# High weights against both halves of x in one product of 512 columns, from up tile 44 on

## The chip, the core and the metric

The kernel runs on one NeuronCore of a Trainium2 chip. Five engines run side by side, each through its own queue in order: TensorE (PE in the profile; its weight loads are listed apart, as PEld), VectorE (DVE), ScalarE (ACT), GpSimd (POOL) and SyncE (SP, which issues the DMAs). They wait for each other by semaphores only. The metric is the device time of one execution in microseconds (us). The kernel before took 2370.12 us, the median of three runs (2369.03 to 2374.41).

## The reference

A decoder trunk of two layers over 256 positions of width 1024. Each layer has a mixer (a gated linear recurrence, an RWKV-7 branch and a latent attention, merged by gates) and then a retrieval over 16,384 experts of one neuron each (PEER), each followed by a residual and a layer norm. The part that matters here is PEER:

```python
q = (xt @ w_query).reshape(T, PEER_HEADS, 2, PEER_HALF)
s1 = jnp.einsum('thd,nd->thn', q[:, :, 0], subkeys[0])
s2 = jnp.einsum('thd,nd->thn', q[:, :, 1], subkeys[1])
...                                    # top 16 of each, top 16 of their sums
gate = jax.nn.softmax(top.astype(jnp.float32), axis=-1).astype(x.dtype)
u = u_table[ib]
vv = v_table[ib]
act = jax.nn.gelu(jnp.einsum('thkd,td->thk', u, xb))
return jnp.einsum('thk,thkd->td', gb * act, vv)
```

All values are float32.

## The kernel before

The kernel gathers nothing: for all 256 tokens it computes the activations of all 16,384 experts, H = gelu(U x), multiplies them by a matrix of gates that is zero outside the chosen experts, and multiplies the result by V. U is 128 "up" tiles of 128 experts, V 128 "down" tiles of 128 experts.

To keep float32 accuracy on TensorE, each operand is split in two float32r halves: hi is the rounded value, lo the remainder. A product is then the sum of three: hi·hi, hi·lo, lo·hi. For x this is done once per layer part (`split`, L165 to L167): the transposed x lies in two SBUF tiles, `xth` and `xtl`, each 128 partitions x 8 blocks x 256 tokens (`new_xt`, L161). For a weight tile it is done on the way in (`stream`, L77 to L90): SP issues a DMA of 512 KB into one of 4 `raw` buffers (L82), ACT casts it to `hi` (L84), and POOL or DVE subtracts `raw - hi` into `lo` (L88); hi and lo have 3 buffers each.

An up tile is `up(e)` (L953): `project` streams the weight tile and issues, for each of 8 blocks k, three matmuls into one PSUM tile `mm` of 128 x 256 (2 banks are set aside for `mm`): L247 hi weights against xth, L248 hi weights against xtl, L249 lo weights against xth. That is 24 matmuls of 256 columns, each with its own weight load. ACT then takes the gelu from PSUM into H (L955). For e < 44 POOL computes lo, from tile 44 on DVE does, since in the first part DVE is busy with the top-16 searches.

From up tile 64 on, `weigh` (L1006) runs beside the up tiles: about every second tile DVE builds 0/1 masks (`oh` L1011, `eq` L1013, `go` L1016), PE multiplies them (16 small matmuls into `sm`, L1020), and DVE multiplies eight tokens' worth of H by the gates (L1023). Then `accumulate` (L253) runs the down tiles: H is split four tiles at a time into `ah2` and `al2` (which take the place of xtl and xth in SBUF, by the tags xb and xa), and each down tile is 12 matmuls of 512 columns (L262) into four PSUM banks `acc`.

Nobody writes the order of instructions out by hand: a scheduler places each engine's instructions by program order and by when buffers come free, and inserts the semaphores. An engine then runs its queue strictly in that order, so that an instruction that waits holds up all that stands behind it.

Of the kernel before, what the change touches and what calls it, by code (L numbers as in the profile page):

```python
# [12 lines left out]
F32R = mybir.dt.float32r  # L13
# [3 lines left out]
AF = mybir.ActivationFunctionType  # L17
# [5 lines left out]
S = 256  # L23
D = 1024
P = 128
# [20 lines left out]
def trunk(ctx, tc, x, xT, w_in, w_br, w_out, w_q, skT, uT, vt, prm, lora, g2, v1, v2, rgw, w_uq, w_ukv,  # L46
          lnp, rope, out):
    nc = tc.nc
    V, A, G, T = nc.vector, nc.scalar, nc.gpsimd, nc.tensor

    const = ctx.enter_context(tc.tile_pool(name="const", bufs=1))
# [6 lines left out]
    def nm(s):  # L58
        uid[0] += 1
        return f"{s}{uid[0]}"  # L60

    def ps(tag, bufs):
        return psum.tile([P, 512], F32, tag=tag, name=nm(tag), bufs=bufs)
# [4 lines left out]
    def pacc():  # L68
        return ps("acc", 4)

    def psm():
        return ps("sm", 2)
# [4 lines left out]
    def stream(src, eng=None, pair=None):  # L77
        if eng is None:
            eng = lo_engine[cnt[0] % len(lo_engine)]
            cnt[0] += 1  # L80
        raw = ring.tile([P, 1024], F32, tag="raw", name=nm("raw"), bufs=NRAW)
        nc.sync.dma_start(raw, src)  # L82
        hi = ring.tile([P, 1024], F32R, tag="hi", name=nm("hi"), bufs=NHI) if pair is None else pair[0]
        A.copy(hi, raw)  # L84
        lo = ring.tile([P, 1024], F32R, tag="lo", name=nm("lo"), bufs=NHI) if pair is None else pair[1]
        n = 512 if eng is G else 1024
        for c in range(0, 1024, n):
            eng.tensor_sub(lo[:, c:c + n], raw[:, c:c + n], hi[:, c:c + n].bitcast(F32))  # L88
        return hi, lo
# [46 lines left out]
    with tc.tile_pool(name="setup", bufs=1) as sb:  # L136
        def t8(n):
            return sb.tile([P, L, 4], F32, tag=n, name=n)
        la = pr[:, :, PC["la"]:PC["la"] + 4]
        ab, e, q, w, w2, acc, rl = (t8(n) for n in ("ab", "e", "q", "w", "w2", "acc", "rl"))  # L140
# [18 lines left out]
    state = {"x": [x[b * P:(b + 1) * P, :] for b in range(2)]}  # L159

    def new_xt():  # L161
        state["xth"] = const.tile([P, 8, S], F32R, tag="xa", name=nm("xth"))
        state["xtl"] = const.tile([P, 8, S], F32R, tag="xb", name=nm("xtl"))

    def split(hi, lo, src, scale=1.0):  # L165
        A.activation(hi, src, AF.Copy, scale=scale)  # L166
# [54 lines left out]
    def finish(b, i, ln, last):  # L221
        if not last:
            if b == 0:
                new_xt()
            transpose_x(b, ln[b])
        nc.sync.dma_start(state["dst"][b], ln[b])
        if b:
            state["x"] = state["dst"]

    def drain(g):  # L230

        while True:
            try:
                next(g)
            except StopIteration as e:
                return e.value

    def project(src, eng=None):
        return drain(projecting(src, eng))

    def projecting(src, eng=None):
        hi, lo = stream(src, eng)
        h3, l3 = hi.rearrange("p (k c) -> p k c", k=8), lo.rearrange("p (k c) -> p k c", k=8)
        pt = pmm()[:, :S]
        xth, xtl = state["xth"], state["xtl"]
        for k in range(8):
            T.matmul(pt, h3[:, k, :], xth[:, k, :], start=(k == 0), stop=False)  # L247
            T.matmul(pt, h3[:, k, :], xtl[:, k, :], start=False, stop=False)  # L248
            T.matmul(pt, l3[:, k, :], xth[:, k, :], start=False, stop=(k == 7))  # L249
            yield  # L250
        return pt
# [638 lines left out]
    def peer(l, hp):  # L890
# [14 lines left out]
        H = [early.enter_context(tc.tile_pool(name=f"h{l}", bufs=1)).tile([P, 64, S], F32, tag="H0", name=nm("H"))]  # L905
# [9 lines left out]
        def nxt(k, lst):  # L915
            cyc[k] = cyc.get(k, -1) + 1
            return lst[cyc[k] % len(lst)]
# [33 lines left out]
            prev = (h, q)  # L951

        def up(e):  # L953
            p = project(uT[l, e], G if e < 44 else V)
            A.activation(H[e // 64][:, e % 64, :], p, AF.Gelu_apprx_tanh)  # L955

        up(0)
        scores(*prev)
        for e in range(1, 24):
            up(e)  # L960
# [18 lines left out]
        for f in range(2):  # L979
            for h4 in range(4):  # L980
                hs = slice(4 * h4, 4 * h4 + 4)
                t = nxt("map", maps)
# [4 lines left out]
        for e in range(24, 44):  # L987
            up(e)
        for b in range(2):
            p = psm()  # L990
# [43 lines left out]
            up(64 + e)  # L1034
            weigh_some(0, e)

        ah2 = const.tile([P, 2, 4, S], F32R, tag="xb", name=nm("ah"))
        al2 = const.tile([P, 2, 4, S], F32R, tag="xa", name=nm("al"))
        last = l == L - 1
        begin_finish(last)  # L1040
        late, ln = ExitStack(), []
# [17 lines left out]
        late.close()  # L1059

    new_xt()
    for q in range(2):
        xt0 = ring.tile([P, 4, S], F32, tag="raw", name=nm("xt0"), bufs=NRAW)
# [72 lines left out]
```

## Time and profile before

| | us |
|---|---|
| runs of the kernel: median (lowest to highest) | 2370.12 (2369.03 to 2374.41) |
| the profiled execution: time on the device | 2366.64 |
| the profiled execution: span from first to last instruction | 2364.9 |
| PE busy in the span | 2261.8 (96%) |
| DVE busy | 1712.3 (72%) |
| ACT busy | 1036.5 (44%) |
| POOL busy | 378.2 (16%) |

The span holds, for each layer, the mixer, the up tiles and the down tiles. In the first layer the up tiles from 44 on and the gates' products lie between about 540 and 799 us, in the second between about 1727 and 1987 us; the down tiles follow until 1168 us and to the end. A busy share of PE says only that a matmul was in flight: matmuls are pipelined, each is shown about 0.28 us long (256 columns) or 0.39 us (512 columns), and the next starts long before that. The distance between two starts is what a matmul costs.

### The profile page before, as it was taken

The page shows a single profiled execution, that of the slowest core. Times are in us where ns is not written, and L with a number is a line of the kernel's source. Part 1 is how long each engine was busy: PE and PEld are TensorE (multiplying, and loading weights), DVE is VectorE, ACT ScalarE, POOL GpSimd, SP SyncE. Part 2 cuts the span into 40 slices and gives each one's busy share as a digit, 9 for nine tenths or more (in the row PEclk, how much of TensorE's full clock was granted, in tenths as well). Part 3 has the DMA queues.
Part 4 walks back from the last instruction along what each step waited for, and adds up shares of the span by engine and source line. Part 5 has one row for each costly group of instructions (what it writes and reads, how often), then busy time and mean ns, then how long its engine had stood idle before and what let it go on. Part 6 is the DMA issues. An engine that isn't in the chain of part 4 may idle for free.

```text
span 2364.9 us, 42121 instructions
## 1 busy us (share of the span) xinstructions
PE 2261.8 (96%) x17092; PEld 2060.4 (87%) x17092; DVE 1712.3 (72%) x3066; ACT 1036.5 (44%) x1461; POOL 378.2 (16%) x284
## 2 busy tenths in 40 slices
PE   7998979999999999999899889799999999999998
PEld 6988969999999988888788789699999999888886
DVE  6888678945777788755676985789446777887556
ACT  4662324444444444444355623244444444444443
POOL 0020017990000000000000100179910000000000
PEclk9998989999999999999999988899999999999999
DMA  5334334455555555656543343345555555556564
GB/s 186 125 126 147 128 109 152 162 177 187 170 168 164 169 178 170 213 194 195 184 142 125 107 131 112 110 145 168 171 187 173 167 167 173 169 170 215 194 191 139
DMA packets 104931, 382.02 MB, mean 162 GB/s; under 512 B 11648, under 2 KB 12160, under 8 KB 104480
## 3 DMA queue, kind: packets, MB, share of 16 engines
q1 hardware_dynamic: 104736, 379.32, 48.9%
q8 instruction: 134, 2.20, 0.4%
q14 instruction: 61, 0.50, 0.1%
HBM read 374.56 MB, written 4.72 MB: 160 GB/s over the span
## 4 chain that ended last, share of the span: by engine, by line
PE 88%; DVE 7%; issue 2%; POOL 2%; ACT 1%; DMA 0%; SPq 0%; DVEq 0%; POOLq 0%; ACTq 0%
PE acc L262 31%; PE mm L247 15%; PE mm L249 15%; PE mm L248 15%; PE sm L1020 3%; DVE lo L88 2%; POOL lo L88 2%; PE acc L812 1%; PE acc L813 1%; PE acc L811 1%; PE sm L932 1%; DVE ti L591 1%; DVE tmp L589 0%; PE sm L298 0%; PE acc L397 0%
## 5 line engine op out<-in xcount | busy, mean ns | idle before, releaser
L84 ACT CAST hi<-raw 128x1024 fp32r<-128x1024 f32 x658 | 689.8, 1049 | 1067.0 <-PE mm L248 439.8
L247 PE MATMUL mm<-xth,hi 128*128 128x256 f32 x3104 | 896.9, 289 | 14.5 <-ACT hi L84 10.9
L249 PE MATMUL mm<-xth,lo 128*128 128x256 f32 x3104 | 891.3, 287 | 15.7 <-POOL lo L88 9.8
L88 DVE TENSOR_TENSOR lo<-raw,hi 128x1024 fp32r<-128x1024 f32 x538 | 660.5, 1228 | 337.3 <-ACT hi L84 335.4
L248 PE MATMUL mm<-xtl,hi 128*128 128x256 f32 x3104 | 887.4, 286 | 0.0
L249 PEld LDWEIGHTS mm<-xth,lo 128*128 128x128 f32 x3104 | 600.5, 194 | 24.7 <-POOL lo L88 14.9
L247 PEld LDWEIGHTS mm<-xth,hi 128*128 128x128 f32 x3104 | 601.8, 194 | 19.9 <-ACT hi L84 10.9
L248 PEld LDWEIGHTS mm<-xtl,hi 128*128 128x128 f32 x3104 | 601.6, 194 | 2.8 <-issue 1.2
L88 POOL TENSOR_TENSOR lo<-raw,hi 128x512 fp32r<-128x512 f32 x240 | 342.8, 1458 | 418.3 <-ACT hi L84 255.1
L262 PE MATMUL acc<-hi,ah 128*128 128x512 f32 x1000 | 316.6, 396 | 0.5 <-ACT ah L166 0.5
L262 PE MATMUL acc<-lo,ah 128*128 128x512 f32 x1000 | 311.7, 391 | 0.0
L262 PE MATMUL acc<-hi,al 128*128 128x512 f32 x1000 | 310.0, 389 | 0.0
L262 PEld LDWEIGHTS acc<-hi,al 128*128 128x128 f32 x1000 | 187.7, 188 | 40.8
L262 PEld LDWEIGHTS acc<-lo,ah 128*128 128x128 f32 x1000 | 187.7, 188 | 40.5 <-DVE lo L88 0.2
L262 PEld LDWEIGHTS acc<-hi,ah 128*128 128x128 f32 x1000 | 183.1, 188 | 34.8 <-ACT ah L166 0.7
L1023 DVE SCALAR_TENSOR_TENSOR H<-sm,H 128x512 f32<-128x512 f32 x128 | 88.3, 690 | 85.1 <-PE sm L1020 84.4
L167 DVE SCALAR_TENSOR_TENSOR al<-H,ah 128x1024 fp32r<-128x1024 f32 x64 | 78.4, 1225 | 42.6 <-ACT ah L166 42.6
L517 POOL MEMSET rmask<- 128x1024 f32 x2 | 1.9, 954 | 663.3 <-DVE xtl L167 646.4
L166 ACT ACTIVATE ah<-H 128x1024 fp32r<-128x1024 f32 x64 | 67.8, 1060 | 80.5 <-PE acc L262 77.1
L1016 DVE TENSOR_TENSOR go<-eq,gp 128x512 f16<-128x512 f16 x256 | 97.3, 418 | 0.0
L955 ACT ACTIVATE H<-mm 128x256 f32<-128x256 f32 x256 | 96.5, 377 | 0.0
L1011 DVE TENSOR_TENSOR oh<-iota,ix 128x1024 f16<-128x1024 f16 x128 | 87.7, 685 | 2.3 <-PE sm L1020 2.3
(352 smaller groups left out, 2131.4 us busy)
## 6 DMA issues: line engine op xcount, KB each, us to landing
raw<-in_uT_dram SPq DMA_DIRECT2D x256, 512.0 KB, 3.4
raw<-in_vt_dram SPq DMA_DIRECT2D x256, 512.0 KB, 3.4
raw<-in_w_in_dram SPq DMA_DIRECT2D x100, 512.0 KB, 3.4
raw<-in_w_q_dram SPq DMA_DIRECT2D x32, 512.0 KB, 3.4
raw<-in_w_br_dram SPq DMA_DIRECT2D x24, 512.0 KB, 3.3
raw<-in_w_out_dram SPq DMA_DIRECT2D x16, 512.0 KB, 3.5
ln<-in_lnp_dram SPq DMA_DIRECT2D x8, 512.0 KB, 5.7
xd<-ln SPq DMA_DIRECT2D x6, 512.0 KB, 2.6
```

What stands on the lines that cost most here:

```text
L84: A.copy(hi, raw)
L88: eng.tensor_sub(lo[:, c:c + n], raw[:, c:c + n], hi[:, c:c + n].bitcast(F32))
L167: V.scalar_tensor_tensor(lo, src, scale, hi.bitcast(F32), op0=OP.mult, op1=OP.subtract)
L247: T.matmul(pt, h3[:, k, :], xth[:, k, :], start=(k == 0), stop=False)
L248: T.matmul(pt, h3[:, k, :], xtl[:, k, :], start=False, stop=False)
L249: T.matmul(pt, l3[:, k, :], xth[:, k, :], start=False, stop=(k == 7))
L262: T.matmul(acc[b][hf], m[:, bs], w[:, 512 * hf:512 * hf + 512], start=(k == 0 and j == 0), stop=(k == n - 1 and j == 2))
L955: A.activation(H[e // 64][:, e % 64, :], p, AF.Gelu_apprx_tanh)
L1011: V.tensor_tensor(oh, iota16[:, None].to_broadcast([P, 8, 64, 2]), ix[:, 1, tt, None, :].to_broadcast([P, 8, 64, 2]), op=OP.is_equal)
L1016: V.tensor_tensor(go[:, i], eq, gp[:, i, tt, None, :].to_broadcast([P, 8, 32, 2]), op=OP.mult)
L1020: T.matmul(p[:, j * 64:(j + 1) * 64], oh[:, j].rearrange("p a b -> p (a b)"), go[:, i, j].rearrange("p a b -> p (a b)"), start=(i == 0), s ...
L1023: V.scalar_tensor_tensor(hv, p.rearrange("p (t e) -> p e t", t=8), 1 / GATE_SCALE, hv, op0=OP.mult, op1=OP.mult)
```

## The change

From up tile 44 on, `up` no longer calls `project`. xth and xtl become the two halves of one tile `xt` (128 x 8 x 2 x 256), so that for each block k the 256 columns of xth and the 256 of xtl lie side by side. The hi weights of a block meet all 512 columns in one matmul (`high`), the lo weights meet the 256 of xth (`low`), whose result is added to the first half of the bank; that makes 8 matmuls of 512 and 8 of 256 columns per tile. The PSUM tile is now one of the four `acc` banks. Its second half holds hi·xtl: ACT copies it into H, DVE adds the first half, and ACT takes the gelu in place. For the same reason ah2 and al2 become halves of one tile under the same tag.

```diff
     def new_xt():
-        state["xth"] = const.tile([P, 8, S], F32R, tag="xa", name=nm("xth"))
-        state["xtl"] = const.tile([P, 8, S], F32R, tag="xb", name=nm("xtl"))
+        xt = state["xt"] = const.tile([P, 8, 2, S], F32R, tag="xab", name=nm("xt"))
+        state["xth"], state["xtl"] = xt[:, :, 0], xt[:, :, 1]
...
         def up(e):
-            p = project(uT[l, e], G if e < 44 else V)
-            A.activation(H[e // 64][:, e % 64, :], p, AF.Gelu_apprx_tanh)
+            if e < 44:
+                p = project(uT[l, e], G if e < 44 else V)
+                A.activation(H[e // 64][:, e % 64, :], p, AF.Gelu_apprx_tanh)
+                return
+
+            hi, lo = stream(uT[l, e], V)
+            h3, l3 = hi.rearrange("p (k c) -> p k c", k=8), lo.rearrange("p (k c) -> p k c", k=8)
+            p, xt = pacc(), state["xt"]
+            for k in range(8):
+                def high():
+                    T.matmul(p, h3[:, k, :], xt[:, k].rearrange("p a t -> p (a t)"), start=(k == 0), stop=(k == 7))
+
+                def low():
+                    T.matmul(p[:, 0:S], l3[:, k, :], xt[:, k, 0], start=False, stop=False)
+
+                for f in ((low, high) if k == 7 else (high, low)):
+                    f()
+            h = H[e // 64][:, e % 64, :]
+            A.copy(h, p[:, S:2 * S])
+            V.tensor_add(h, h, p[:, 0:S])
+            A.activation(h, h, AF.Gelu_apprx_tanh)
...
-        ah2 = const.tile([P, 2, 4, S], F32R, tag="xb", name=nm("ah"))
-        al2 = const.tile([P, 2, 4, S], F32R, tag="xa", name=nm("al"))
+        a2 = const.tile([P, 2, 2, 4, S], F32R, tag="xab", name=nm("a2"))
+        ah2, al2 = a2[:, 0], a2[:, 1]
```

On PE, two blocks k of an up tile in the first layer stood like this (mm is the tile's PSUM sum, hi and lo its weights):

```order
L247 MATMUL mm_6064<-xth_3551,hi_6060 128x256
L248 MATMUL mm_6064<-xtl_3552,hi_6060 128x256
L249 MATMUL mm_6064<-xth_3551,lo_6062 128x256
L247 MATMUL mm_6064<-xth_3551,hi_6060 128x256
L248 MATMUL mm_6064<-xtl_3552,hi_6060 128x256
L249 MATMUL mm_6064<-xth_3551,lo_6062 128x256
```

and of an up tile past 44 in the changed kernel, from its first block on (L964 is `high`, L967 is `low`):

```order
L964 MATMUL acc_6116<-xt_3550,hi_6112 128x512
L967 MATMUL acc_6116<-xt_3550,lo_6114 128x256
L964 MATMUL acc_6116<-xt_3550,hi_6112 128x512
L967 MATMUL acc_6116<-xt_3550,lo_6114 128x256
L964 MATMUL acc_6116<-xt_3550,hi_6112 128x512
L967 MATMUL acc_6116<-xt_3550,lo_6114 128x256
```

Three matmuls per block became two, with the same 768 columns.

On DVE, one period of two up tiles past tile 64 stood like this in the first layer (L1023 applies the gates, L88 makes lo of an up tile three ahead, oh, go and eq are the masks):

```order
L1023 SCALAR_TENSOR_TENSOR H_3591<-sm_6909,H_3591 128x64x8
L88 TENSOR_TENSOR lo_7020<-raw_7016,hi_7018 128x1024
L1011 TENSOR_TENSOR oh_7080<-iota_5923,ix_5925 128x1024
L1016 TENSOR_TENSOR go_7082<-eq_7081,gp_5927 128x512 x2
L1013 TENSOR_TENSOR eq_7227<-iota_5923,ix_5925 128x512
L88 TENSOR_TENSOR lo_7052<-raw_7048,hi_7050 128x1024
L1023 SCALAR_TENSOR_TENSOR H_3591<-sm_6998,H_3591 128x64x8
```

and so in the changed kernel (L973 is the added sum; L1042, L1030, L1035 and L1032 are L1023, L1011, L1016 and L1013 of before; acc_6789, acc_6840, acc_6866 and then the tile of lo_6915 follow each other on PE):

```order
L973 TENSOR_TENSOR H_6448<-H_6448,acc_6789 128x256
L1042 SCALAR_TENSOR_TENSOR H_3589<-sm_6816,H_3589 128x64x8
L88 TENSOR_TENSOR lo_6915<-raw_6911,hi_6913 128x1024
L1030 TENSOR_TENSOR oh_6886<-iota_5921,ix_5923 128x1024
L1035 TENSOR_TENSOR go_6888<-eq_6887,gp_5925 128x512 x2
L973 TENSOR_TENSOR H_6448<-H_6448,acc_6840 128x256
L1032 TENSOR_TENSOR eq_7092<-iota_5921,ix_5923 128x512
L88 TENSOR_TENSOR lo_6941<-raw_6937,hi_6939 128x1024
L973 TENSOR_TENSOR H_6448<-H_6448,acc_6866 128x256
```

The sum of tile n stands ahead of lo of tile n + 3; the rest kept its order. On ACT the copy of tile n now stands ahead of the cast of tile n + 3, and the gelu of tile n behind it. POOL and SP kept their order.

## Rows read from the trace of the kernel before

**Rows 1.** The page: engines' busy time, share of the span, instructions

```profile
PE 2261.8 (96%) x17092; PEld 2060.4 (87%) x17092; DVE 1712.3 (72%) x3066; ACT 1036.5 (44%) x1461; POOL 378.2 (16%) x284
```

**Rows 2.** The page: the chain that ended last, by engine and by line

```profile
PE 88%; DVE 7%; issue 2%; POOL 2%; ACT 1%; DMA 0%; SPq 0%; DVEq 0%; POOLq 0%; ACTq 0%
PE acc L262 31%; PE mm L247 15%; PE mm L249 15%; PE mm L248 15%; PE sm L1020 3%; DVE lo L88 2%; POOL lo L88 2%; PE acc L812 1%; PE acc L813 1%; PE acc L811 1%; PE sm L932 1%; DVE ti L591 1%; DVE tmp L589 0%; PE sm L298 0%; PE acc L397 0%
```

**Rows 3.** Busy us by stretch: length, PE, PEld, DVE, ACT, POOL, clock, DMA, GB/s

```profile
548.00:602.00 54.00, 54.00 (x453) 54.00 (x452) 24.07 (x23) 25.25 (x38) 0.00 (x0) 1.00 0.58 187
606.00:798.00 192.00, 192.00 (x1955) 190.67 (x1954) 146.00 (x220) 81.15 (x122) 0.00 (x0) 1.00 0.52 167
1792.00:1984.00 192.00, 192.00 (x1955) 190.67 (x1954) 147.15 (x220) 79.85 (x121) 0.00 (x0) 1.00 0.51 167
```

**Rows 4.** Groups by line, 606 to 798 us: busy, mean ns, idle before

```profile
L88 DVE TENSOR_TENSOR lo<-raw,hi 128x1024 fp32r<-128x1024 f32 x61 | 74.4, 1220 | 13.2 <-ACT hi L84 13.2
L84 ACT CAST hi<-raw 128x1024 fp32r<-128x1024 f32 x61 | 64.0, 1049 | 112.2 <-PE mm L248 112.2
L1023 DVE SCALAR_TENSOR_TENSOR H<-sm,H 128x512 f32<-128x512 f32 x31 | 21.4, 690 | 31.7 <-PE sm L1020 31.7
```

**Rows 5.** Timeline, PE: start us, us, instruction, at an up tile's end

```profile
619.85 0.28 PE L247 MATMUL mm<-xth,hi 128*128 128x256 f32 x1
...
621.77 0.28 PE L248 MATMUL mm<-xtl,hi 128*128 128x256 f32 x1
621.89 0.28 PE L249 MATMUL mm<-xth,lo 128*128 128x256 f32 x1
622.01 0.64 PE L1020 MATMUL sm<-go,oh 128*128 128x64 f16 x16
...
622.68 0.28 PE L248 MATMUL mm<-xtl,hi 128*128 128x256 f32 x1
```

**Rows 6.** Chain in order of time, down tiles of the first layer

```profile
982.57 185.37 PE acc L262 x816
```

**Rows 7.** Timeline, DVE, one period past tile 64, with idle before

```profile
620.28 1.23 DVE L88 TENSOR_TENSOR lo<-raw,hi 128x1024 fp32r<-128x1024 f32 x1 [0.36 <-ACT hi L84]
622.68 0.69 DVE L1023 SCALAR_TENSOR_TENSOR H<-sm,H 128x512 f32<-128x512 f32 x1 [1.17 <-PE sm L1020]
623.29 1.22 DVE L88 TENSOR_TENSOR lo<-raw,hi 128x1024 fp32r<-128x1024 f32 x1
624.42 0.69 DVE L1011 TENSOR_TENSOR oh<-iota,ix 128x1024 f16<-128x1024 f16 x1
625.03 0.75 DVE L1016 TENSOR_TENSOR go<-eq,gp 128x512 f16<-128x512 f16 x2
625.81 0.42 DVE L1013 TENSOR_TENSOR eq<-iota,ix 128x512 f16<-128x512 f16 x1
626.60 1.23 DVE L88 TENSOR_TENSOR lo<-raw,hi 128x1024 fp32r<-128x1024 f32 x1 [0.36 <-ACT hi L84]
```

**Rows 8.** Timeline, ACT, behind the end of the same up tile

```profile
622.09 1.05 ACT L84 CAST hi<-raw 128x1024 fp32r<-128x1024 f32 x1 [1.55 <-PE mm L248]
623.04 0.38 ACT L955 ACTIVATE H<-mm 128x256 f32<-128x256 f32 x1
```

**Rows 9.** Groups by line, whole span: nearest to copy and sum

```profile
L948 ACT COPY tk<-mm 128x256 f32<-128x256 f32 x32 | 11.7, 365 | 0.0
L817 DVE SCALAR_TENSOR_TENSOR gt<-gt,acc 128x256 f32<-128x256 f32 x16 | 6.7, 418 | 3.5 <-PE acc L813 3.4
L940 DVE TENSOR_TENSOR tk<-tk 128x256 f32<-128x256 f32 x32 | 27.6, 861 | 0.0
```

**Rows 10.** Timeline from the last up tile to the first down tile

```profile
799.33 0.96 PE L1020 MATMUL sm<-go,oh 128*128 128x64 f16 x27
799.41 1.06 ACT L166 ACTIVATE ah<-H 128x1024 fp32r<-128x1024 f32 x1 [1.55 <-PE mm L248]
...
800.52 0.50 PE L262 MATMUL acc<-hi,ah 128*128 128x512 f32 x1 [0.23 <-ACT ah L166]
```

## The prediction

> **What bounds the kernel now.** First the page's table of engines: PE is busy for 96% of the span, DVE for 72%, ACT for 44% [rows 1]. The chain that ended last agrees: 88% of it is PE, 45% the three projection lines L247 to L249, DVE 7% [rows 2]. Shares over the span hide stages, so the next view is the busy time by stretch. Within the changed part PE has no idle time: 54.00 of 54 us among tiles 44 to 63, 192.00 of 192 us among tiles 64 to 127, in both layers alike, at granted clock 1.00, the 2.4 GHz level [rows 3]. DVE is at 45% and then 76%, ACT at 47% and 42%, POOL is idle. The groups by line say who waits for whom: the casts wait for PE's matmuls (112.2 us), DVE's L1023 for PE's gate products (31.7 us), lo for the cast (13.2 us) [rows 4]. So everyone waits for PE here, and only PE's own time counts, as long as the others keep up.
>
> What a matmul costs is the distance of starts. With 256 columns, 16 starts take from 619.85 to 621.77 us: 120 ns each [rows 5]. With 512 columns, 816 matmuls of the down tiles take 185.37 us, of which the last one's shown length is 0.39: 184.98 / 815 = 227 ns [rows 6]. Two products of 256 columns cost 240 ns, one of 512 costs 227: 13 ns go with the instruction and not with its columns.
>
> **The change, part by part.**
> *PE, the matmuls.* A tile before: 24 x 0.120 = 2.880 us. After: 8 x 0.227 + 8 x 0.120 = 2.776 us. 104 ns less per tile, for 84 tiles in each of two layers: 168 x 0.104 = 17.5 us less. No row shows 512 and 256 columns taking turns, so the block's price is bounded from both sides. Above: the long one costs as much as two short ones, 360 ns as before, gain 0. Below: nothing but columns, 768 at the granted 2.4 GHz = 320 ns (an estimate from the clock of rows 3), 8 x 40 = 320 ns a tile, 53.8 us in all. I take 347, since both spacings stand in the trace over long unbroken stretches.
>
> The rows put 13 ns on each matmul beside its columns. The Trainium skill (TensorE: Matmul & The Clock Gate, section Back-to-back issue gap) gives columns / 2.4 + 2.5 ns between isolated matmuls at the full clock, that is 109 and 216 ns. By that rule the change would save an estimated 2.5 ns x 8 x 168 = 3.4 us, so it speaks against the change; the trace does not agree with it, at 120 and 227 ns.
>
> *ACT.* Per tile it gains a copy of 128 x 256 out of PSUM, 0.37 us by the nearest row (L948, 365 ns) [rows 9], and its gelu now reads SBUF instead of PSUM; I leave it at 0.38 [rows 8]. 0.37 + 1.05 + 0.38 = 1.80 us in 2.78: free of charge, hidden under PE.
>
> *DVE.* Per tile it gains a sum of 128 x 256 with one operand in PSUM. The nearest rows are 418 ns (L817, PSUM, same size) and, far off, 861 ns (L940, same size, both operands in SBUF and another shape of access) [rows 9]; from below no more than nothing. I take 0.42, since L817 reads PSUM in the same shape. In the period of two tiles DVE works without a gap from 622.68 to 626.23 (625.81 + 0.42), 3.55 us, and on one more lo of 1.23: 4.78 us; it waits 1.17 and 0.36 [rows 7]. With two sums 5.62. The new period on PE is 2 x 2.776 plus the gate product, 0.55 (622.01 to the 622.56 that lies one step ahead of the L248 at 622.68) [rows 5] = 6.10 us. DVE fits, at 92%.
>
> *The added waits.* The sum of tile n waits for ACT's copy, which waits for the last matmul of n. Behind it on DVE stand, in the order shown with the change, L1042 of the gate product and lo of tile n + 3; behind the gelu on ACT stands the next copy. Let tile n leave PE at 0. Its last matmul, shown 0.39 long, ends at 0.16; the cast of before began 0.04 after the shown end of the last L248 (621.77 + 0.28, 622.09) [rows 5, 8], so the copy runs from 0.20 to 0.57, the cast of n + 3 to about 1.6, the sum from 0.6 to 1.0. L1042 to 1.6, lo of n + 3 to 2.8, the masks to 4.15. The copy of n + 1 is done at 0.55 + 2.78 + 0.57 = 3.90, its sum ends at 4.57, the mask eq and lo of n + 4 (cast done at 4.9) end at 6.1. The next sum could not start before 6.10 + 0.60 = 6.70: DVE still idles 0.6 us per period. PE needs lo of n + 3 at 6.65 + 0.23 and lo of n + 4 at 9.4: 3 to 4 us in hand. lo of n + 3 could not be early anyway, since its buffer is that of tile n (three buffers), which is why the casts waited for PE before. So the waits cost nothing; without this cover each would cost 0.6 us a tile. PSUM: four acc banks instead of two mm banks, freed 1.0 us after a tile leaves PE; no wait.
>
> *DMA.* The order on SP did not move; raw buffers come free with lo, as before. 512 KB per 2.78 us instead of 2.88 is 4% more than the 187 GB/s of tiles 44 to 63 at a DMA share of 0.58 [rows 3]: hidden.
>
> *The seam to the down tiles.* The first split (ah) waited for the last L248 and began 0.08 us after tile 127 left PE at 799.33; the first down matmul came at 800.52, after 0.23 us idle [rows 10]. Now ACT does the copy of tile 127 first: ah from about 0.55 to 1.6, and the down tiles begin 1.63 instead of 1.19 us after the last up tile. Cost 0.44, twice: 0.9 us, bounded by 0 (if gate products fill it) and 2 x 1.2. xt and a2 now share one buffer, but both halves were released at the same end before.
>
> *Sum.* -17.5 + 0.9 = -16.6 us. The profiled execution took 2366.64 us (span 2364.9 and 1.7 around it) and would take 2350.0. It lies 3.5 us below the median of the runs, 2370.12; the forecast for a median is 2370.1 - 16.6 = 2353.5 us.
>
> **The rivals.**
> *No gain on PE (B).* The 13 ns may belong to the succession and not to the instruction: now each long product must cover the load of the low weights and each short one that of the high weights, and a stream that takes turns may fall back to 360 ns per block. For it: no row shows the mix, and PEld was at 99% of these stretches [rows 3]. Against it: loads are as many per matmul as before, and both pure streams carry the same 13 ns. Time 2370.1 + 0.9 = 2371. By the rule of the Trainium skill named above (TensorE: Matmul & The Clock Gate, section Back-to-back issue gap) it would be an estimated 2370.1 - 3.4 + 0.9 = 2367.6 us.
>
> *A larger gain (C).* If at 256 columns it is the weight load that sets 120 ns, then fewer loads free more: down to 320 ns per block, 2370.1 - 53.8 + 0.9 = 2317. For it: the loads fill PEld at 256 columns. Against it: at 512 columns, where loads have twice the room, the same 13 ns remain.
>
> *DVE becomes the bound (D, slower).* Place: tiles 64 to 127, 32 periods in each layer. The sum decides: above (6.10 - 4.78) / 2 = 0.66 us each, DVE is longer than PE and PE starts to wait for lo; above about 0.8 the loss eats what tiles 44 to 63 win (40 x 0.104 = 4.2). At L940's 0.86 the period is 4.78 + 1.72 = 6.50 instead of the present 6.32: 64 x 0.18 = 11.5 us lost, 2370.1 + 11.5 - 4.2 + 0.9 = 2378. If besides DVE's present waits (1.17 + 0.36) stayed on top of 5.62, the period would be 7.15 and the time 2420. For it: 92% in a queue that now waits twice more per period. Against it: these waits end with a tile whose successors' lo is already made, and L817's 418 ns is the same access.
>
> **How the numbers follow.** Forecast 77%, its own range 2349 to 2358 us (block price by 2 ns, seam, scatter of the runs); B 9%, C 5%, D 9%. About 0.2%, 4.7 us, is what a measurement of this kernel can tell from no change. Faster by more than that: the forecast and C, 82%. Within it: B, 9%. Slower: D, 9%. The range for 8 times in 10 takes the forecast and nearly all of B, and leaves C and D out: 2346 to 2371 us.
>
> **What would show it.** Right: in the stretch of tiles 44 to 127 PE is without idle time, L964 starts are followed after 227 ns and L967 after 120, so that a block takes 347 ns; DVE is near 90% in tiles 64 to 127 with the sum at about 0.42 us and still idle once per period, before the odd tile's sum, and the first down tile starts some 9 us earlier in the first layer and 17 in the second. Wrong: a block at 360 (B) or near 320 (C), or idle time of PE before L967 that ends with DVE's lo, with DVE never idle (D).

## The result, and the profile after

The changed kernel takes 2353.45 us (median of 8 runs, 2350.16 to 2358.08), the kernel before, run beside it, 2368.31 us (8 runs, 2357.90 to 2374.41). The ratio is 0.9939, 95% interval 0.9926 to 0.9952: 14.4 us less, between 11.4 and 17.5. The forecast was 2353.5 us. (One of all executions here, of experiment 1, ran at a granted clock of 0.83, took 2498.69 us and is left out of that experiment's ratio.) The profiled execution of the changed kernel took 2351.38 us, 15.3 less than that of before.

Line numbers of the changed kernel: L964 is the long product (512 columns), L967 the short one, L972 ACT's copy, L973 DVE's sum, L974 the gelu, L1042 the gate product's multiplication, L1011 the transposes just ahead of tile 44.

Engines on the page, against [rows 1]: 1344 matmuls fewer, PE still at 96%, DVE up from 72 to 75%.

```profile
PE 2247.3 (96%) x15748; PEld 1982.4 (84%) x15748; DVE 1764.3 (75%) x3234; ACT 1089.2 (46%) x1629; POOL 378.6 (16%) x284
```

Busy time by stretch (length, PE, PEld, DVE, ACT, POOL, clock, DMA share, GB/s), against [rows 3]: PE still has no idle time in the changed part, at granted clock 1.00. PEld fell from 99 to 87%, DVE rose from 76 to 88%.

```profile
548.00:600.00 52.00, 52.00 (x297) 45.21 (x296) 33.71 (x48) 30.46 (x56) 0.00 (x0) 1.00 0.56 184
604.00:788.00 184.00, 184.00 (x1465) 159.58 (x1465) 161.69 (x275) 97.88 (x180) 0.00 (x0) 1.00 0.53 172
1775.00:1965.00 190.00, 190.00 (x1499) 164.89 (x1498) 166.23 (x284) 101.56 (x186) 0.00 (x0) 1.00 0.52 172
```

Groups by line from 604 to 788 us, against [rows 4, 9]: no idle time ahead of L964 or L967. The copy costs 373 ns, the sum 417. The sum waits 18.0 us for the copy, no row shows a wait for the sum; L1042, 31.7 us idle before, now never waits.

```profile
L964 PE MATMUL acc<-xt,hi 128*128 128x512 f32 x477 | 170.1, 399 | 0.0
L967 PE MATMUL acc<-xt,lo 128*128 128x256 f32 x476 | 123.4, 279 | 0.0
L88 DVE TENSOR_TENSOR lo<-raw,hi 128x1024 fp32r<-128x1024 f32 x60 | 73.5, 1224 | 4.9 <-ACT hi L84 4.9
L973 DVE TENSOR_TENSOR H<-H,acc 128x256 f32<-128x256 f32 x60 | 25.0, 417 | 18.0 <-ACT H L972 18.0
L972 ACT COPY H<-acc 128x256 f32<-128x256 f32 x60 | 22.4, 373 | 86.8 <-PE acc L964 86.8
L1042 DVE SCALAR_TENSOR_TENSOR H<-sm,H 128x512 f32<-128x512 f32 x32 | 21.9, 684 | 0.0
```

DVE's timeline of one period answers to [rows 7]: idle time is left twice, 0.18 and 0.64 us.

```profile
620.16 1.23 DVE L88 TENSOR_TENSOR lo<-raw,hi 128x1024 fp32r<-128x1024 f32 x1
...
622.57 0.41 DVE L973 TENSOR_TENSOR H<-H,acc 128x256 f32<-128x256 f32 x1
622.90 0.42 DVE L1032 TENSOR_TENSOR eq<-iota,ix 128x512 f16<-128x512 f16 x1
623.51 1.23 DVE L88 TENSOR_TENSOR lo<-raw,hi 128x1024 fp32r<-128x1024 f32 x1 [0.18 <-ACT hi L84]
625.37 0.42 DVE L973 TENSOR_TENSOR H<-H,acc 128x256 f32<-128x256 f32 x1 [0.64 <-ACT H L972]
```

PE's timeline, two pieces of neighbouring tiles, answers to [rows 5]: blocks (a long and a short product) take 346 to 347 ns in the first (from 619.87, 620.22, 620.56), 349 to 361 in the second (from 622.65, 623.01, 623.36; the view rounds to 10 ns). The forecast had 347 everywhere.

```profile
619.87 0.39 PE L964 MATMUL acc<-xt,hi 128*128 128x512 f32 x1
620.10 0.28 PE L967 MATMUL acc<-xt,lo 128*128 128x256 f32 x1
620.22 0.39 PE L964 MATMUL acc<-xt,hi 128*128 128x512 f32 x1
620.45 0.28 PE L967 MATMUL acc<-xt,lo 128*128 128x256 f32 x1
620.56 0.39 PE L964 MATMUL acc<-xt,hi 128*128 128x512 f32 x1
...
622.65 0.40 PE L964 MATMUL acc<-xt,hi 128*128 128x512 f32 x1
622.89 0.28 PE L967 MATMUL acc<-xt,lo 128*128 128x256 f32 x1
623.01 0.40 PE L964 MATMUL acc<-xt,hi 128*128 128x512 f32 x1
623.25 0.28 PE L967 MATMUL acc<-xt,lo 128*128 128x256 f32 x1
623.36 0.40 PE L964 MATMUL acc<-xt,hi 128*128 128x512 f32 x1
```

**Where the time went.** The stretch from the transposes to the first down matmul holds all that was changed. Before, it ran from 539.05 to 800.52 us and from 1726.61 to 1988.07, 261.47 and 261.46 us; the same two rows of after, with the last gate products between them:

```profile
543.63 0.82 PE L1011 MATMUL sm<-ident,tk 128*128 128x128 f32 x6
...
797.42 1.11 PE L1039 MATMUL sm<-go,oh 128*128 128x64 f16 x32
799.00 0.50 PE L262 MATMUL acc<-hi,a 128*128 128x512 f32 x1 [0.47 <-ACT a L166]
```

255.37 us, and 255.37 again in layer 2 (1717.74 to 1973.11): 12.2 us less in both. The other 3.1 of the 15.3 us between the two profiled executions lie where the two programs do the same work: the first layer reaches its transposes 4.6 us later, the second needs 7.4 us less from its first down matmul to its transposes in the next layer, the end 0.3 less. The granted clock in such stretches changes from execution to execution (0 to 340 us: 0.96 before, 0.94 after), and the time goes with it: among the profiles of this case that do the same work up to there, the first transposes come at 537.6 to 539.1 us where that clock was 0.96, and at 542.7 to 544.8 us where it was 0.94. So the stretch, which repeats within 0.1 us, is the measure in what follows, and 12.2 us lies within the interval of the runs. One thing more moves in it: of a layer's 1024 small gate products (128x64, some 30 ns each) it holds 539 before and 544 after.

### The profile page after: what moved, and what is told of

Same layout as the page of the kernel before. It is cut to its first block, busy times and chain, and to the rows that moved or that the text cites. A ratio compares the mean times of both kernels' runs of the same rounds, so it can differ in the third digit from the quotient of the medians.

```text
span 2349.7 us, 39919 instructions
## 1 busy us (share of the span) xinstructions
PE 2247.3 (96%) x15748; PEld 1982.4 (84%) x15748; DVE 1764.3 (75%) x3234; ACT 1089.2 (46%) x1629; POOL 378.6 (16%) x284
## 4 chain that ended last, share of the span: by engine, by line
PE 87%; DVE 7%; POOL 2%; issue 2%; ACT 1%; DMA 0%; SPq 0%; DVEq 0%; POOLq 0%; ACTq 0%
PE acc L262 31%; PE acc L964 13%; PE mm L249 8%; PE mm L247 8%; PE mm L248 8%; PE acc L967 7%; PE sm L1039 3%; POOL lo L88 2%; DVE lo L88 2%; PE acc L812 1%; PE sm L932 1%; PE acc L811 1%; PE acc L813 1%; PE sm L298 0%; DVE ti L591 0%
## 5 line engine op out<-in xcount | busy, mean ns | idle before, releaser
L88 DVE TENSOR_TENSOR lo<-raw,hi 128x1024 fp32r<-128x1024 f32 x538 | 659.9, 1227 | 277.1 <-ACT hi L84 275.2
L262 PE MATMUL acc<-hi,a 128*128 128x512 f32 x2000 | 554.7, 392 | 0.9 <-ACT a L166 0.9
L249 PE MATMUL mm<-xt,lo 128*128 128x256 f32 x1760 | 512.8, 292 | 15.7 <-POOL lo L88 9.7
L247 PE MATMUL mm<-xt,hi 128*128 128x256 f32 x1760 | 512.9, 292 | 15.2 <-ACT hi L84 11.6
L248 PE MATMUL mm<-xt,hi 128*128 128x256 f32 x1760 | 509.1, 289 | 0.0
L964 PE MATMUL acc<-xt,hi 128*128 128x512 f32 x1344 | 474.3, 399 | 0.0
L262 PEld LDWEIGHTS acc<-hi,a 128*128 128x128 f32 x2000 | 370.9, 188 | 76.3 <-ACT a L166 1.2
L88 POOL TENSOR_TENSOR lo<-raw,hi 128x512 fp32r<-128x512 f32 x240 | 343.2, 1460 | 415.9 <-DVE lo L88 329.3
L249 PEld LDWEIGHTS mm<-xt,lo 128*128 128x128 f32 x1760 | 344.6, 196 | 24.5 <-POOL lo L88 14.9
L247 PEld LDWEIGHTS mm<-xt,hi 128*128 128x128 f32 x1760 | 345.6, 197 | 20.6 <-ACT hi L84 11.6
L967 PE MATMUL acc<-xt,lo 128*128 128x256 f32 x1344 | 348.6, 280 | 0.0
L248 PEld LDWEIGHTS mm<-xt,hi 128*128 128x128 f32 x1760 | 345.3, 196 | 2.8 <-issue 1.2
L262 PE MATMUL acc<-lo,a 128*128 128x512 f32 x1000 | 311.2, 391 | 0.0
L964 PEld LDWEIGHTS acc<-xt,hi 128*128 128x128 f32 x1344 | 245.4, 188 | 44.4
L967 PEld LDWEIGHTS acc<-xt,lo 128*128 128x128 f32 x1344 | 253.5, 189 | 12.1
L972 ACT COPY H<-acc 128x256 f32<-128x256 f32 x168 | 62.7, 373 | 231.2 <-PE acc L964 231.2
L973 DVE TENSOR_TENSOR H<-H,acc 128x256 f32<-128x256 f32 x168 | 70.1, 418 | 60.6 <-ACT H L972 60.6
```

The costliest lines, as they stand in the source:

```text
L262: T.matmul(acc[b][hf], m[:, bs], w[:, 512 * hf:512 * hf + 512], start=(k == 0 and j == 0), stop=(k == n - 1 and j == 2))
L964: T.matmul(p, h3[:, k, :], xt[:, k].rearrange("p a t -> p (a t)"), start=(k == 0), stop=(k == 7))
L967: T.matmul(p[:, 0:S], l3[:, k, :], xt[:, k, 0], start=False, stop=False)
L973: V.tensor_add(h, h, p[:, 0:S])
```

## The experiments

The theory behind the prediction: PE pays 13 ns per instruction beside its columns, the copy, the sum and the waits cost nothing. Open after the result: why a tile took 2.80 us in the mean and not 2.776, and how near DVE was to the bound. "Stretch" is the one above, layer 1 / layer 2.

**1. Old products, new copy and sum.**

```diff
             for k in range(8):
-                ...                              # high and low, as in the change
+                T.matmul(p[:, 0:S], h3[:, k, :], xt[:, k, 0], start=(k == 0), stop=False)
+                T.matmul(p[:, 0:S], l3[:, k, :], xt[:, k, 0], start=False, stop=(k == 7))
+            for k in range(8):
+                T.matmul(p[:, S:2 * S], h3[:, k, :], xt[:, k, 1], start=(k == 0), stop=(k == 7))
```

> The changed kernel's two halves of the bank, its copy by ACT and its sum on DVE stay, but the products are the old ones: per k three matmuls of 256 columns (high weights with the high half of x and low weights with the high half into the first half of the bank, high weights with the low half of x into the second), 24 per tile instead of 16. Theory (the gain comes from fewer matmul instructions alone, copy and sum cost PE nothing): a tile takes 2.88 us as before, the stretch from the transposes to the first down matmul 261.47 + 0.44 = 261.9 us per layer (before 261.47, after 255.37), the time that of before plus 0.9, 2369 us. Rival 1 (copy and sum, which read the bank while PE writes the next, slow PE, and that is the 44 ns per tile by which the changed kernel fell short of 2.776 us): a tile of 2.92 us, 261.9 + 84 x 0.044 = 265.6 us per layer, 2376 us. Rival 2 (the gain comes from elsewhere, for instance the merged buffer of x): 255.4 us per layer, 2354 us.

Measured: 261.84 / 261.85 us, ratio to before 1.0009 (0.9998 to 1.0021). With 24 products instead of 16 the whole gain is gone, and copy, sum, waits and the merged buffer together cost 0.37 to 0.39 us per layer. PE's rows show a tile of 2.88 us (569.09 to 571.97) and the down tiles 1.57 us behind the end of the last up tile (the start of the gate products that follow it) instead of 1.19 [rows 10], so that is the seam, forecast at 0.44, and nothing else.

```profile
569.09 1.12 PE L966 MATMUL acc<-xt,hi 128*128 128x256 f32 x8
...
571.97 1.12 PE L966 MATMUL acc<-xt,hi 128*128 128x256 f32 x8
```

**2. No copy and no sum.**

```diff
-            A.copy(h, p[:, S:2 * S])
-            V.tensor_add(h, h, p[:, 0:S])
-            A.activation(h, h, AF.Gelu_apprx_tanh)
+            A.activation(h, p[:, 0:S], AF.Gelu_apprx_tanh)
```

> The changed kernel without copy and sum: gelu reads the first half of the bank directly (the products of the low half of x are computed and left out of the output). The matmuls are those of the changed kernel. If copy and sum slow PE (side work): tiles of 2.776 us, 261.47 - 84 x 0.104 = 252.7 us from the transposes to the first down matmul, without the seam's 0.44. If the succession of long and short products or the bank sets it: tiles stay at 2.78 to 2.83 us, and the stretch takes 255.4 - 0.4 = 255.0 us. DVE falls to about 75% of tiles 64 to 127.

Measured: 255.36 / 255.34 us, and tiles 44 to 63, timed at the seventh of their 16 products, alternate between 2.81 and 2.83 us as in the changed kernel. The missing 27 ns per tile (2.803 us in the mean instead of 2.776) don't come from copy or sum. DVE fell to 79% of tiles 64 to 127, where 75% were expected. (The expected seam of 0.4 less did not show: here ACT did the gelu ahead of the first split instead of the copy.)

**3. Batched: seven long products, eight short ones, the last long one.**

> The same sixteen products per tile, but seven long ones in a row, then the eight short ones, then the last long one, so that long and short follow each other 2 times per tile instead of 16 times. If taking turns costs the missing 44 ns per tile: tiles of 2.776 to 2.785 us, 261.47 - 8.7 + 0.44 = 253.2 us from the transposes to the first down matmul, 2.2 us per layer less than the changed kernel, 2349 us. If the side work or the bank costs it: 2.78 to 2.83 us per tile and 255.4 us as in the changed kernel, 2353 us.

```diff
+            for k in range(7):
+                T.matmul(p, h3[:, k, :], xt[:, k].rearrange("p a t -> p (a t)"), start=(k == 0), stop=False)
             for k in range(8):
-                ...                              # high and low in turns
+                T.matmul(p[:, 0:S], l3[:, k, :], xt[:, k, 0], start=False, stop=False)
+            T.matmul(p, h3[:, 7, :], xt[:, 7].rearrange("p a t -> p (a t)"), start=False, stop=True)
```

Measured: 254.59 / 254.57 us, 2355.75 us, ratio 0.9945 (0.9924 to 0.9966). Between the two expectations: 0.8 us per layer is won, 1.4 more were expected. A tile of PE's timeline says what the products cost:

```profile
570.25 1.77 PE L963 MATMUL acc<-xt,hi 128*128 128x512 f32 x7
571.86 1.11 PE L965 MATMUL acc<-xt,lo 128*128 128x256 f32 x8
572.81 0.40 PE L966 MATMUL acc<-xt,hi 128*128 128x512 f32 x1
```

Seven long ones from 570.25 to 571.86 are 230 ns each, eight short ones to 572.81 are 119. The long product costs 230 here in the mean, where [rows 6] had 227.

The mean hides a start. A tile of number 8, which has the same order, stands in two windows that both show the end of the same seven long products:

```profile
1700.74 1.54 PE L963 MATMUL acc<-xt,hi 128*128 128x512 f32 x6
```

```profile
1701.67 0.84 PE L963 MATMUL acc<-xt,hi 128*128 128x512 f32 x3
1702.35 1.11 PE L965 MATMUL acc<-xt,lo 128*128 128x256 f32 x8
```

The first four of the seven, to 1701.67, are 232 ns each, the last three, to 1702.35, are 227. To the nanosecond, the starts of long products that follow short ones are 233, 236, 228, 233 and 231 ns apart and only then 226 to 227, the value of [rows 6]; the first short ones behind long ones are 113 and 119 ns apart, the others 120. In number 3 the steps are the same within 1 ns. So it is not the stage that sets 230, but the change of length ahead of the row.

**4. Other banks: the up sums in the two banks of the narrow projections.**

```diff
-            p, xt = pacc(), state["xt"]
+            p, xt = pmm(), state["xt"]
```

> The changed kernel with the up tiles' sums in the two banks of the narrow projections (mm) instead of the four wide ones (acc). In the changed kernel tiles take turns at about 2.78 and 2.82 us, and the turn flips where two gate products follow each other, so it goes with the tile's number. If the bank sets it: with other banks the pattern changes (all tiles at 2.78 or all at 2.82), the stretch takes 253.5 to 257 us. If it is the succession or the side work: 255.4 us and the same pattern. If two banks are too few, PE waits ahead of a tile's first long product for the sum that frees the bank, 1.0 us after the tile before the last one has left: no idle time expected, since a tile of 2.8 us lies between.

Measured: 255.42 / 255.36 us, the same pattern of tiles. The choice of bank sets neither the time nor the pattern.

**5. The sum done twice, and 11. three times.**

```diff
             V.tensor_add(h, h, p[:, 0:S])
+            V.tensor_add(h, h, p[:, 0:S])    # in 11 this line stands twice
```

> The changed kernel with the sum on DVE done twice (0.83 instead of 0.42 us per tile; its output holds the first half of the bank twice). A test of the threshold of the prediction's rival D: DVE's work per period of two tiles and one gate product is 4.78 + 4 x 0.417 = 6.45 us against PE's 6.16 (3.345 + 2.81 as measured in the changed kernel). If DVE's busy time alone decides: 32 periods x 0.29 = 9.4 us more per layer, 264.8 us from the transposes to the first down matmul, 18.9 us more in all, 2372 us, slower than before. If DVE's present waits for ACT's copy (0.64 us per period) stay on top: 32 x 0.93 = 30 us per layer, 285 us, 2413 us. If the period has more room than that sum says: 255.4 us and 2353 us. Tiles 44 to 63 stay at 2.82 us in each case.

Measured: 255.36 / 255.33 us, 2352.59 us, ratio 0.9927 (0.9912 to 0.9942). 0.83 us of sums per tile instead of 0.42 cost nothing. DVE's timeline shows why (start, shown length):

```profile
619.61 0.42 DVE L973 TENSOR_TENSOR H<-H,acc 128x256 f32<-128x256 f32 x1 [0.26 <-ACT H L972]
619.95 0.69 DVE L1043 SCALAR_TENSOR_TENSOR H<-sm,H 128x512 f32<-128x512 f32 x1
620.55 0.41 DVE L974 TENSOR_TENSOR H<-H,acc 128x256 f32<-128x256 f32 x1
620.88 1.22 DVE L88 TENSOR_TENSOR lo<-raw,hi 128x1024 fp32r<-128x1024 f32 x1
622.01 0.69 DVE L1031 TENSOR_TENSOR oh<-iota,ix 128x1024 f16<-128x1024 f16 x1
```

The sum starts at 619.61 and the next instruction at 619.95: 0.34 us of DVE's time, not 0.42. The second sum: 0.33, lo: 1.13. Shown lengths overlap by some 0.08 us, so adding them up made DVE too full. The busy share hides it too: DVE is busy for 178.14 of 184 us, 97%, and still PE does not wait.

```profile
604.00:788.00 184.00, 184.00 (x1452) 159.64 (x1451) 178.14 (x336) 104.33 (x180) 0.00 (x0) 1.00 0.52 170
```

> The changed kernel with the sum on DVE done three times (its output holds the first half of the bank three times). Done twice it cost nothing (255.36 us per layer), since DVE's instructions follow each other 0.08 us sooner than their shown lengths say: the sum takes 0.335 us of DVE's time, a period 4.62 + 6 x 0.335 = 6.63 us against PE's 6.16. If DVE's distances of starts decide: 32 x 0.47 = 15 us more per layer, 270.4 us from the transposes to the first down matmul, 2383 us in all. If DVE has still more room: 255.4 us. If the waits for ACT's copy come on top (0.25 us per period were left): 278 us, 2399 us.

Measured (three sums): 270.91 / 270.95 us, 2389.61 us in one run. The 270.4 of the distances of starts is met within 0.6 (within 1.5 if one counts the 32 gate products, some 1 us, that here stand behind the first down matmul), and this is rival D: PE idles 6.1 us of the 184 and waits for lo.

```profile
604.00:788.00 184.00, 177.90 (x1348) 148.40 (x1347) 179.75 (x356) 91.19 (x165) 0.00 (x0) 1.00 0.50 155
```

```profile
PEld acc L967 <- DVE lo L88: 7.8, 22, 1.0
...
PE acc L967 <- DVE lo L88: 2.9, 6, 0.6
PEld acc L964 <- ACT hi L84: 2.4, 3, 0.8
```

(The second group: who waited for whom, us in total, times, longest.) That it came so close is partly luck. By the distances of starts in numbers 5 and 11, DVE's work of a period without sums is 4.5 us (lo twice 1.14, the gates' product and oh 0.60 each, go twice 0.34, eq 0.34), not 4.78 and not the 4.62 of the expectation; with six sums that makes 6.5 us. The other 0.15 us of a period is DVE's own idle time (4.25 of the 184 us, 3.4 of it behind ACT's copy), which the expectation had left out. DVE would become the bound at an estimated (6.16 - 4.5) / 2 = 0.83 us of distance per sum, 0.91 as shown, not at 0.66; the runs themselves show only that two sums (0.67) cost nothing and three (1.0) cost 15.6 us per layer.

**6. Batched, odd k into a second bank** (half of the terms left out).

```diff
-            p, xt = pacc(), state["xt"]
+            ps2, xt = (pacc(), pacc()), state["xt"]
             for k in range(8):
+                T.matmul(ps2[k % 2], h3[:, k, :], xt[:, k].rearrange("p a t -> p (a t)"), start=(k < 2), stop=False)
+            for k in range(8):
+                T.matmul(ps2[k % 2][:, 0:S], l3[:, k, :], xt[:, k, 0], start=False, stop=(k > 5))
...
```

> The products batched (eight long ones, then eight short ones), and each odd k goes to a second bank, so that successive products never write the same bank (copy reads one bank and the sum the other, so half of the terms are left out of the output). The long product measured 230 ns in the batched order where all write one bank; the 227 ns of the prediction came from down tiles, whose successive products write different banks. If the bank sets the difference: long ones 227 ns, tiles of 2.77 to 2.78 us, 252.9 us from the transposes to the first down matmul. If it is the kind of operand or the work beside it: 2.79 us and 254.6 us as in the batched kernel.

Measured: 254.61 / 254.61 us. Eight long ones from 570.62 to 572.46 are again 230 ns each in the mean, with the same steps as in number 3.

```profile
570.62 2.00 PE L963 MATMUL acc<-xt,hi 128*128 128x512 f32 x8
572.46 1.12 PE L965 MATMUL acc<-xt,lo 128*128 128x256 f32 x8
```

**7. Down tiles, three products in a row into one bank.**

```diff
-            for j, (m, w) in enumerate(((mh, wh), (mh, wl), (ml, wh))):
-                for hf in hfs:
+            for hf in hfs:
+                for j, (m, w) in enumerate(((mh, wh), (mh, wl), (ml, wh))):
```

> The changed kernel with the down tiles' products in another order: the three products of a half of the columns follow each other in one bank, where before and in the changed kernel two banks take turns. If writing the same bank in succession costs 3 to 4 ns per long product: the stretch without gate products behind 982 us runs at 230 instead of 227 ns, 1464 products of 512 columns per layer cost 4 to 5 us more, 2 x 4.5 = 9 us in all, 2362 us. If not: 227 ns and 2353 us. The up tiles stay at 255.4 us.

Measured: 2349.29 us in one run, and the stretch of [rows 6] unchanged. With 6 this excludes the bank as the reason for 230 against 227.

```profile
980.79 185.37 PE acc L262 x816
```

**9. and 10. Other operands for the long product**, batched (the edit stands against number 3): in 9 it streams 512 columns of the high weights, in 10 it also loads 128 columns of x.

```diff
             for k in range(7):
-                T.matmul(p, h3[:, k, :], xt[:, k].rearrange("p a t -> p (a t)"), start=(k == 0), stop=False)
+                T.matmul(p, h3[:, k, :], hi[:, 0:512], start=(k == 0), stop=False)            # 9
+                T.matmul(p, xt[:, k, 0, 0:P], hi[:, 0:512], start=(k == 0), stop=False)       # 10
...                                              # the last long product likewise
```

> The batched order; the long product streams 512 columns of the tile's own high weights instead of the two halves of x (so the up sums are not those of the reference). The long product cost 230 ns in tiles 44 to 127 and 227 in the down tiles, in any bank. If the place of the streamed operand (the buffer of x, read by every tile) makes the 3.5 ns: 227 ns, tiles of 2.77 us, 253.0 us from the transposes to the first down matmul. If not: 254.6 us.

> The batched order; the long product loads 128 columns of x and streams 512 columns of the high weights, as the down tiles do with their operands (the up sums are not those of the reference). If which operand is loaded and which is streamed makes the 3.5 ns: 227 ns, tiles of 2.77 us, 253.0 us per layer. If it is the stage or the long row of products in itself: 254.6 us.

Measured: 254.09 / 254.09 and 254.59 / 254.60 us. Neither won anything in the up tiles: from the transposes to the end of tile 127 both take 253.01 to 253.02 us, number 3 253.00 to 253.02. The 0.5 us of number 9 lies at the seam, where the scheduler put 24 instead of 32 gate products ahead of the first down matmul and PE idles 0.20 instead of 0.47 us. So neither the place nor the role of the operands explains 230 against 227.

**12. Pairs: two long, two short.**

```diff
-                for f in ((low, high) if k == 7 else (high, low)):
-                    f()
+                for f, j in (((high, k), (high, k + 1), (low, k), (low, k + 1)) if k < 6 else
+                             ((high, k), (low, k), (low, k + 1), (high, k + 1))):
+                    f(j)
```

> The changed kernel with two long products, then two short ones, and so on, half as many turns between the two lengths as in the changed kernel. One turn per product gave 2.82 us per tile and 255.37 us per layer, two turns per tile 2.793 and 254.58. If each turn costs the same: half-way, 2.805 us and 255.0 us. If only strict taking of turns costs: 254.6 us.

Measured: 256.47 / 256.47 us, 1.1 more than with strict turns. Both expectations fell for the stretch as a whole. Up to the first gate product the order is as the first of them had it: 22 tiles take 62.08 us with strict turns, 61.97 in pairs, 61.55 batched. All that pairs lose, some 1.2 us, they lose behind that, where gate products stand between the tiles; why is not shown.

**8. Batched, and the change from tile 34 on.**

```diff
-            if e < 44:
-                p = project(uT[l, e], G if e < 44 else V)
+            if e < 34:
+                p = project(uT[l, e], G)
...                                              # and the order of number 3
```

> The batched order, and the change from up tile 34 on instead of 44 (lo of tiles 34 to 43 on DVE instead of POOL, which has no gap there). DVE has finished the routing before tile 34. Theory (16 instead of 24 matmuls pay wherever PE is the bound): 20 tiles more x 0.09 us = 1.8 us, and what PE idles for POOL's lo between tiles 34 and 43, at most 1.7 us per layer, so 2 to 5 us; with the 1.6 us of the batched order 2347 to 2351 us, ratio to before 0.992. Rival (POOL's or DVE's order sets tiles 34 to 43, so the gain is lost in waits for the routing): 2352 us as the batched order alone.

Measured: 2351.09 us, ratio to before 0.9914 (0.9901 to 0.9928), the lowest ratio of all, though its interval still touches that of the change as made (0.9926 to 0.9952). Tiles 34 to 43 run from the first long product to the transposes in 27.95 us instead of 10 x 2.88, 0.85 us less per layer, and PE has no idle time there.

```profile
509.00 1.78 PE L963 MATMUL acc<-xt,hi 128*128 128x512 f32 x7
...
536.95 0.82 PE L1007 MATMUL sm<-ident,tk 128*128 128x128 f32 x6
```

With the batched order that makes 12.2 + 1.6 + 1.7 = 15.5 us against before by the stretches; the interval of the runs, 17 to 23.5 us, lies above that. The profiled execution took 18.4 us less than that of before, 2.9 of it in stretches that the edit did not touch. The routing on DVE was done by then; PE's 4.9 us of waits for POOL's lo, in the tiles ahead, stay.

## Why the prediction was right, and where it was not

- *The bound and the mechanism*: right. PE sets the stage, and fewer instructions at equal columns pay. Number 1 shows it: with copy and sum but 24 products the gain is gone. Each product here has its own weight load, so the runs don't tell whether the product or its load costs the 13 ns.
- *The block at 347 ns*: mis-sized. It averaged 350.3: the stretch fell by 6.10 us, with the seam's 0.39 back 6.49, over 84 tiles 77 ns per tile instead of 104. That is 13.0 us instead of 17.5 on 168 tiles. The step that was off took the two spacings from unbroken streams and added them. They don't hold behind a change of length (numbers 3, 6 and 8): batched, the first five long products of a row cost 25 ns more a tile than 227 each, the first two short ones together some 8 less than 120 each, so that a tile takes 2.793 us. With strict turns the price never settles: up to the first gate product long ones are 235 ns apart and short ones 117 in the mean, a tile takes 2.82 us, over all 84 tiles 2.803. The bounds, 320 to 360, held the value.
- *Rival B, a block at 360*: wrong as a whole, but its argument that turns may cost something was right for 27 of the 104 ns per tile that the forecast counted on.
- *Rival B, by the Trainium skill (TensorE: Matmul & The Clock Gate, section Back-to-back issue gap)*: its columns / 2.4 + 2.5 ns made an estimated gain of 3.4 us. The stretches lost 12.2, so the trace does not agree with it.
- *Copy and its waits on ACT, DMA*: right, hidden. Number 1 leaves no room for a cost beside the seam.
- *The seam*: 0.44 forecast, 0.37 to 0.39 measured. Only 0.24 of it is PE's idle time (0.23 before, 0.47 after); the rest is five more gate products, 32 instead of 27, ahead of the first down matmul.
- *The sum on DVE*: 0.42 forecast, 0.417 measured. The room beside it was too small in the working: shown lengths were added where distances of starts count. DVE idled 0.82 us per period (0.64 and 0.18), not 0.6. Rival D had its mechanism right (number 11) and its threshold wrong: L940's 861 ns would have stayed below the estimated 0.91, and cost nothing by that estimate instead of 11.5 us.
- *First down tile 9 us earlier in layer 1, 17 in layer 2*: it came 1.5 and 15.0 us earlier. Unchanged work ahead of it moved by +4.6 us in layer 1, three quarters of a stage's gain; taken from the transposes on, the step was 6.1 us in each layer.
- *The time*: 2353.5 against 2353.45. That it meets so closely is partly chance: by the stretches 12.2 us less was due, the forecast said 16.6, and the runs give 11.4 to 17.5. The medians fell by 14.9, and the kernel before, run again, took 2368.31 us and not the 2370.1 from which the forecast started; the two differences of 1.7 and 1.8 us cancel.

## What to carry to other kernels

Where PE has no gap, merge products with the same weights into one long product: the gain comes with each product (and its weight load) that is saved, but price it from a row with the same succession of lengths: 227 ns held from the sixth long product of a row on, and turns took a quarter of the gain away. Whether a second engine has room is read from distances of starts, not from shown lengths or busy shares. For a change under 1% compare a stretch between two marks that holds the change, and count what else lies in it (here the gate products); it repeats within 0.1 us while the whole scattered by 8 us (after) and 16 (before).

## What the runs showed of the hardware beside that

- DVE's instructions in a row start some 0.08 us before the shown end of the one before: 97% busy, and PE did not wait (number 5).
- The 512-column product ran at 227 ns in the up tiles and in the down tiles, in any bank and with either role of the operands, once five of its kind had gone ahead; the first five behind 256-column products were 228 to 236 ns apart. The down tiles of the kernel before show the same behind 16 gate products of 64 columns: one distance of 315 ns, nine of 224 to 236, then 226 to 227. What makes the start dearer stays open.
- Strict turns of 512 and 256 columns gave tiles of 2.78 to 2.83 us in a pattern of two, which flips where two gate products follow each other and is the same with other banks and without copy and sum.
